# Staggered start addresses modulo 128 bytes for weight slots and activation tiles

## The chip, the cores and the metric

The kernel runs on one NeuronCore of one Trainium2 chip. The metric is the device time of one launch, in microseconds (us), taken as the median of several runs. Five engines take part: PE (TensorE, matrix products, with the loads of its stationary operand listed apart as PEld), DVE (VectorE), ACT (ScalarE), POOL (GpSimd) and SP (SyncE, which here only issues DMAs). A matmul reads two operands from SBUF: the stationary one (`lhsT`), which is loaded first, and the moving one (`rhs`), which is then streamed through.

## The reference

Two layers of a transformer block on 256 tokens with 1,024 features. Every layer is: half a SwiGLU feed-forward block, three mixers side by side (a gated MLP, a retention and a sparse attention), and a second half feed-forward block. Cut to what matters:

```python
def swiglu_ffn(x, w1, w2):
    a, b = jnp.split(x @ w1, 2, axis=-1)
    return (jax.nn.silu(a) * b) @ w2

for l in range(DEPTH):                                   # 2 layers
    x = x + 0.5 * swiglu_ffn(rms_norm(x, ffn1_norm[l]), ffn1_w1[l], ffn1_w2[l])
    h = rms_norm(x, mix_norm[l])
    proj = h @ w_in[l]                                   # 1024 -> 3864
    ...                                                  # y_a, y_b, y_c: the three mixers
    mix = g_a * (y_a @ w_out[0]) + g_b * (y_b @ w_out[1]) + g_c * (y_c @ w_out[2])
    x = x + mix @ w_o[l]
    x = x + 0.5 * swiglu_ffn(rms_norm(x, ffn2_norm[l]), ffn2_w1[l], ffn2_w2[l])
return rms_norm(x, final_norm)
```

The feed-forward width is 2,816 (22 blocks of 128). All is float32.

## The kernel before

Activations stand with the features on the 128 partitions and the 256 tokens along the free axis. To keep float32 accuracy on a faster matmul form (`float32r`), each factor is split in two: `hi` is its value rounded to float32r, `lo` what is left over. A product is then three matmuls: weight-hi by activation-hi, weight-hi by activation-lo, weight-lo by activation-hi.

**Weights.** `issue` (L206) brings the weights in pieces of up to 128 x 1024 floats: SP issues the DMA into a slot `raw` (4 slots of 4,096 bytes per partition), ACT copies it to `hi` (L219), and DVE and POOL share the subtraction that gives `lo` (L223). Both halves lie in one slot `hl` (4 slots of 8,192 bytes per partition: `hi`, then `lo` 4,096 bytes on). `piece` (L229) hands a piece out and keeps three more on their way.

**Activations.** `x16` (L112) gives a tile `xhl` for eight blocks of 128 features, `hi` first and `lo` 8,192 bytes on (2 slots of 16,384 bytes); the normed input of every stage lies in one. `s8` (L105) gives a tile for four blocks (6 slots of 8,192 bytes; the profile calls them `s`): the hidden blocks of the feed-forward, the mixers' outputs and several scratch tiles.

**Matmul helpers.** All of them go through `mm` (L147), so the profile puts all of them at L148.
- `mm_feat` (L240): stationary a weight block of 128 columns, moving 256 tokens; three matmuls of 256 columns per block.
- `mm_wide` (L259): the same with the two matmuls that share weight-hi taken as one of 512 columns, whose moving operand has two rows of 256 (`hi` and `lo`); so one matmul of 512 and one of 256 per block. Most of the feed-forward runs so.
- `mm_tok` (L274): the roles are swapped: stationary are 128 tokens of the activation, moving are the weights, 256 or 280 columns at a time. In `tok` (L902) with 280 columns a weight block begins every 280 x 4 = 1,120 bytes in its slot, and the pieces hold 3, 3 and 2 blocks; every block is used for both halves of the tokens, three matmuls each.
- `hidden` (L616): stationary are 60 columns of a scratch tile, moving are weights, two rows of 128.

**Order.** PE's instructions stand in the order in which the program writes them; the other engines' order is set by the scheduler. Small steps of the mixers (`unit`, `compress`, `retention` and others) are generators that run between the large products.

**Where tiles begin.** The allocator puts the slots of a pool one behind the other. By the built program, these are the places (start modulo 128 bytes) at which they begin:

| tile | slots | before | after |
|---|---|---|---|
| `raw` | 4 | 32 32 32 32 | the same |
| `hl` | 4 | 32 32 32 32 | 32 64 96 0 |
| `xhl` | 2 | 64 64 | 64 96 |
| `s` (by `s8`) | 6 | 64 64 64 64 64 64 | 0 32 64 96 0 32, each with 0 or 16 more by turns |
| `ph` | 2 | 96 96 | 96 96 |
| `ks` | 1 | 64 | 64 |

The 128-column blocks of a weight piece (512 bytes), the 256-token blocks of an activation (1,024 bytes) and the distances from `hi` to `lo` are multiples of 128 bytes, so they begin at their tile's place. The 280-column blocks don't: their three blocks begin at 32, 0 and 96 modulo 128.

Of the kernel before, what the change touches and what calls it, by code (L numbers as in the profile page):

```python
# [7 lines left out]
F32 = mybir.dt.float32  # L8
F32R = mybir.dt.float32r
# [12 lines left out]
GS = 0.21145921592590802  # L22
W2_SPLIT = (8, 8, 6)
SLOT = 1024

AHEAD = 3
FFN_SPLIT = 7
# [39 lines left out]
def tile_hybrid_block(  # L67
# [22 lines left out]
    ring = ctx.enter_context(tc.tile_pool(name="ring", bufs=1))  # L90
    act = ctx.enter_context(tc.tile_pool(name="act", bufs=1))
    ps = ctx.enter_context(tc.tile_pool(name="ps", bufs=1, space=PSUM))
    ctx.enter_context(tc.manual_schedule(engines={mybir.EngineType.PE}))
    uid = [0]

    def nm(s):
        uid[0] += 1
        return f"{s}_{uid[0]}"
# [4 lines left out]
        return t  # L103

    def s8(dt=F32R):  # L105
        return act.tile([128, 2, 4, 256], dt, tag="s8", name=nm("s8"), bufs=6)

    def flat8(dt=F32):
        t = s8(dt)
        return [t[:, i].rearrange("p a b -> p (a b)") for i in range(2)]  # L110

    def x16():  # L112
        return act.tile([128, 2, 8, 256], F32R, tag="xhl", name=nm("xhl"), bufs=2)

    def t2(tag="t2", bufs=6):
        return act.tile([128, 512], F32, tag=tag, name=nm(tag), bufs=bufs)

    def small(n, tag="small", bufs=17):
        return act.tile([128, n], F32, tag=tag, name=nm(tag), bufs=bufs)

    def pmm():
        return ps.tile([128, 512], F32, tag="mm", name=nm("mm"), bufs=2)

    def psc():
        return ps.tile([128, 512], F32, tag="sc", name=nm("sc"), bufs=3)
# [4 lines left out]
    def pms():  # L130
        return ps.tile([128, 512], F32, tag="ms", name=nm("ms"), bufs=2)

    def soon():

        return tc.high_priority(offset=EARLY)
# [11 lines left out]
    def mm(o, lhsT, rhs, start, stop):  # L147
        nc.tensor.matmul(o, lhsT=lhsT, rhs=rhs, start=start, stop=stop)  # L148
        n = 1
        for d in rhs.shape[1:]:  # L150
            n *= d
        if lhsT.dtype == F32R:
            clk[0] += max(n / 2400.0, 0.107) + 0.0025
        else:
            clk[0] += max(4 * n / 2400.0, 0.214)

    def transpose(o, i):
        nc.tensor.transpose(o, i, ident)  # L158
        clk[0] += 0.109
# [46 lines left out]
    def issue(cuts=1, between=None):  # L206
        kn, n = specs[len(queue)]
        raw = ring.tile([128, SLOT], F32, tag="raw", name=nm("raw"), bufs=4)
        hl = ring.tile([128, 2, SLOT], F32R, tag="hl", name=nm("hl"), bufs=4)
        hi, lo = hl[:, 0], hl[:, 1]  # L210
        o, m = woff[0], kn * n
        woff[0] += 128 * m
        src = w[o:o + 128 * m].rearrange("(p f) -> p f", p=128)
        for c in range(cuts):
            if between:
                between(c)
            s_ = slice(c * m // cuts, (c + 1) * m // cuts)
            nc.sync.dma_start(raw[:, s_], src[:, s_])
            S.copy(hi[:, s_], raw[:, s_])  # L219
            cut = m if cuts > 1 else (kn * pool_lo[0] // 8) * n  # L220
            for e, a, b in ((V, s_.start, min(cut, s_.stop)), (G, max(cut, s_.start), s_.stop)):
                if a < b:
                    e.tensor_tensor(out=lo[:, a:b], in0=raw[:, a:b], in1=hi[:, a:b].bitcast(F32), op=ALU.subtract)  # L223
        w3 = hl[:, :, :m].rearrange("p c (k n) -> p c k n", n=n)
        queue.append([w3[:, :, k] for k in range(kn)])
# [81 lines left out]
    def norm_begin(i):  # L307
        st = {"i": i, "n": 0, "q": []}
        if i < 6:
            hl = x16()  # L310
            st["h"], st["l"] = hl[:, 0], hl[:, 1]
            st["a"] = [hl[:, :, k] for k in range(8)]
        st["acc"] = act.tile([128, 256], F32, tag="acc", name=nm("acc"), bufs=1)
        return st
# [75 lines left out]
    def ffn(st, nxt, first=False, load=None):  # L390
# [3 lines left out]
        def evac(j, p):  # L394
            R2 = st["R"][:, None, :].to_broadcast([128, 2, 256])
            if j % 4 == 0:
                t4[:] = [s8()]
            h4, l4 = t4[0][:, 0], t4[0][:, 1]
            t, u = t2(), t2()
            t3 = t.rearrange("p (a b) -> p a b", a=2)  # L400
            if isinstance(p, list):
                for n in range(2):
                    S.copy(t3[:, n], p[n][:, 256:512])  # L403
                    V.tensor_tensor(out=t3[:, n], in0=p[n][:, 0:256], in1=t3[:, n], op=ALU.add)  # L404
                V.tensor_tensor(out=t3, in0=t3, in1=R2, op=ALU.mult)  # L405
            elif isinstance(p, tuple):
                for n in range(2):
                    V.tensor_tensor(out=t3[:, n], in0=p[n][:, 0:256], in1=st["R"], op=ALU.mult)
            else:
                V.tensor_tensor(out=t3, in0=p.rearrange("p (a b) -> p a b", a=2), in1=R2, op=ALU.mult)  # L410
            S.activation(u[:, 0:256], t[:, 0:256], AF.Silu)  # L411
            V.tensor_tensor(out=u[:, 256:512], in0=u[:, 0:256], in1=t[:, 256:512], op=ALU.mult)  # L412
            S.copy(h4[:, j % 4], u[:, 256:512])
            V.tensor_tensor(out=l4[:, j % 4], in0=u[:, 256:512], in1=h4[:, j % 4].bitcast(F32), op=ALU.subtract)  # L414
            hs.append(t4[0][:, :, j % 4])
# [91 lines left out]
    def mixer(l, st, nxt):  # L507
        a = st["a"]
# [38 lines left out]
        def has(*names):  # L547
            return lambda: all(n in ev for n in names)
# [167 lines left out]
        def cmp_branch(qt):  # L716
            yield has(f"s{qt}0", f"s{qt}1")
            sc = scs[qt]
            s3 = sc.rearrange("p (h n) -> p h n", n=16)
            mx = small(8)  # L720
            V.tensor_reduce(out=mx, in_=s3, axis=AX.X, op=ALU.max)
            V.tensor_tensor(out=s3, in0=s3, in1=mx[:, :, None].to_broadcast([128, 8, 16]), op=ALU.subtract)
            S.activation(sc, sc, AF.Exp)
            yield 2.0
            V.tensor_tensor(out=sc, in0=sc, in1=ccmp[:, 1, qt].rearrange("p j g n -> p (j g n)"), op=ALU.mult)
            sm = small(8)
            V.tensor_reduce(out=sm, in_=s3, axis=AX.X, op=ALU.add)
            V.tensor_scalar(sm, sm, 1e-30, None, op0=ALU.max)
            V.reciprocal(sm, sm)
            V.tensor_tensor(out=sm.rearrange("p (j g) -> p g j", g=2), in0=sm.rearrange("p (j g) -> p g j", g=2),  # L730
                            in1=gate[qt][:, :, 0].rearrange("p (g j) -> p g j", g=2), op=ALU.mult)
            V.tensor_tensor(out=s3, in0=s3, in1=sm[:, :, None].to_broadcast([128, 8, 16]), op=ALU.mult)
            yield WAIT_CB
            p = pms()
            transpose(p[:, 0:128], sc)
            ct = act.tile([128, 128], F32, tag="sct", name=nm("sct"), bufs=1)
            S.copy(ct, p[:, 0:128])
            yield 3.0
            yield has(f"u{qt}0", f"u{qt}1", "yalloc")
            o, p = os[qt], pms()  # L740
            for j in range(4):
                mm(p[:, j * 128:j * 128 + 128], lhsT=VC[:, j], rhs=ct, start=True, stop=True)
            qs = slice(qt * 128, qt * 128 + 128)
            o3 = o.rearrange("p (j t) -> p j t", j=4)
            with soon():
                V.tensor_tensor(out=o, in0=o, in1=p, op=ALU.add)
                S.copy(yh[2][:, :, qs], o3)
                V.tensor_tensor(out=yl[2][:, :, qs], in0=o3, in1=yh[2][:, :, qs].bitcast(F32), op=ALU.subtract)
            ev.add(f"yc{qt}")
# [270 lines left out]
        def outs(pairs, wks, alloc=pmm):  # L1020
            p = alloc()
            for n, (b, d) in enumerate(pairs):
                yield from mm_feat(p[:, n * 256:n * 256 + 256], wks[n], [yt[b][:, :, k] for k in range(4)], True, True)
            return p
# [3 lines left out]
        for d in range(8):  # L1028
# [6 lines left out]
            p = yield from outs(((0, d), (1, d)), (wk[0:4], wk[4:8]))  # L1035
# [14 lines left out]
        for d in range(0, 8, 2):  # L1050
# [10 lines left out]
            if d < 6:  # L1061
                p = yield from outs(((2, d), (2, d + 1)), (wk[0:4], wk[4:8]), psc)
# [6 lines left out]
            else:  # L1069
                u = t2()  # L1070
                for n in range(2):
                    p = yield from outs(((2, d + n),), (wk[4 * n:4 * n + 4],), psc)
# [8 lines left out]
        p = (pmm()[:, 0:256], psc()[:, 0:256])  # L1081
# [3 lines left out]
        for d in range(2, 8):  # L1085
            p = pmm()
            f, o = (mm_wide, p) if d < WIDE else (mm_feat, p[:, 0:256])
# [29 lines left out]
    for k, n in ((0, 1), (1, 2), (3, 2), (5, 2), (7, 1)):  # L1117
        t = t2()[:, 0:n * 256].rearrange("p (a b) -> p a b", b=256)
# [143 lines left out]
```

## Time and profile before

| | us |
|---|---|
| median of 3 runs (1267.82 to 1269.81) | 1268.05 |
| the profiled execution, its own time | 1271.46 |
| its span, first to last instruction | 1269.6 |
| PE busy in it | 1243.8 (98%) |
| DVE, ACT, POOL busy | 987.2, 718.6, 447.4 |

Busy time of PE counts a matmul from its start to its modelled end, and matmuls overlap, so a busy PE may still run at different paces. The pace is read from starts: from the start of one group of matmuls to the start of the next, divided by the matmuls in it.

### The profile page before, as it was taken

What the parts mean: (1) busy time and instruction counts of PE and PEld (TensorE: products, weight loads), DVE (VectorE), ACT (ScalarE), POOL (GpSimd) and SP (SyncE); (2) the same over time, 40 slices, a digit from 0 to 9 for tenths busy, and PEclk for the clock granted to TensorE, in tenths of its full rate; (3) what the DMA queues carried; (4) which work ended last, traced back from release to release, by engine and by line L of the source; (5) the groups of instructions that cost most, each with busy time, mean ns of one, the idle gap of its engine ahead of it and who ended that gap; (6) DMA issues with size and microseconds to landing.
All of it is one profiled execution on the core that took longest, in us unless ns stands there. A gap on an engine that the chain in (4) does not pass through costs nothing.

```text
span 1269.6 us, 22596 instructions
## 1 busy us (share of the span) xinstructions
PE 1243.8 (98%) x8440; PEld 1152.0 (91%) x8440; DVE 987.2 (78%) x1636; ACT 718.6 (57%) x1232; POOL 447.4 (35%) x419
## 2 busy tenths in 40 slices
PE   9999999998999999999999999999999999999997
PEld 9888899998998988888998888999999988888886
DVE  6988776789875888887778886686997758788863
ACT  6666445567764556564455654465676644666542
POOL 0533230264554733331213322203635548133222
PEclk9999999999998999999999999999999989999998
DMA  8855666644553555556555556575445545556562
GB/s 286 262 197 181 184 198 206 220 155 146 166 161 123 177 188 190 191 179 194 191 185 197 186 183 190 176 240 179 146 149 156 162 130 170 184 190 192 185 185 78
DMA packets 68957, 230.44 MB, mean 182 GB/s; under 512 B 8816, under 2 KB 11504, under 8 KB 68848
## 3 DMA queue, kind: packets, MB, share of 16 engines
q1 hardware_dynamic: 68256, 227.90, 55.8%
q0 software_dynamic: 448, 1.08, 0.3%
q8 instruction: 66, 1.08, 0.3%
q14 instruction: 43, 0.35, 0.1%
q10 hardware_dynamic: 144, 0.03, 0.0%
HBM read 225.80 MB, written 1.05 MB: 179 GB/s over the span
## 4 chain that ended last, share of the span: by engine, by line
PE 84%; DVE 5%; POOL 4%; ACT 3%; issue 2%; DMA 1%; SPq 0%; POOLq 0%; DVEq 0%; ACTq 0%
PE mm L148 58%; PE sc L148 23%; DVE hl L223 2%; PE ms L148 2%; POOL hl L223 1%; ACT hl L219 1%; POOL acc L345 1%; POOL sq L341 1%; PE o L148 1%; PE sc L158 1%; DMA raw<-in_w_dram 1%; ACT P L667 0%; ACT t L819 0%; DMA x<-in_x_dram 0%; POOL rs L794 0%
## 5 line engine op out<-in xcount | busy, mean ns | idle before, releaser
L223 DVE TENSOR_TENSOR hl<-raw,hl 128x896 fp32r<-128x896 f32 (+6 forms) x437 | 501.0, 1149 | 160.4 <-ACT hl L219 158.9
L219 ACT CAST hl<-raw 128x1024 fp32r<-128x1024 f32 (+3 forms) x437 | 443.5, 1018 | 283.7 <-PE mm L148 186.6
L148 PE MATMUL mm<-xhl,hl 128*128 128x256 f32 (+1 forms) x3784 | 561.0, 303 | 1.1 <-ACT hl L219 0.5
L148 PEld LDWEIGHTS mm<-xhl,hl 128*128 128x128 f32 x3784 | 507.5, 189 | 32.1 <-issue 1.4
L223 POOL TENSOR_TENSOR hl<-raw,hl 128x128 fp32r<-128x128 f32 (+2 forms) x264 | 309.1, 1172 | 487.3 <-ACT hl L219 458.1
L148 PE MATMUL mm<-s,hl 128*128 128x512 f32 (+1 forms) x1880 | 294.7, 317 | 0.0
L148 PEld LDWEIGHTS mm<-s,hl 128*128 128x128 f32 x1880 | 266.3, 188 | 25.9
L148 PE MATMUL sc<-xhl,hl 128*128 128x256 f32 (+1 forms) x1560 | 275.3, 328 | 0.1
L148 PEld LDWEIGHTS sc<-xhl,hl 128*128 128x128 f32 x1560 | 232.9, 189 | 25.9 <-DVE hl L223 0.3
L403 ACT COPY t<-sc 128x256 f32<-128x256 f32 x81 | 30.3, 374 | 90.3 <-PE sc L148 90.3
L341 POOL TENSOR_TENSOR sq<-x 128x256 f32<-128x256 f32 x36 | 25.0, 696 | 134.7 <-DVE x L386 134.7
L148 PE MATMUL mm<-hl,xhl 128*128 128x256 f32 (+1 forms) x432 | 59.9, 289 | 0.0
L405 DVE TENSOR_TENSOR t<-t,R 128x512 f32<-128x512 f32 x81 | 56.2, 694 | 2.8
L414 DVE TENSOR_TENSOR s<-t,s 128x256 fp32r<-128x256 f32 x88 | 56.7, 645 | 0.0
L148 PEld LDWEIGHTS mm<-hl,xhl 128*128 128x128 f32 x432 | 54.5, 188 | 2.2 <-issue 1.9
L345 POOL TENSOR_TENSOR acc<-acc,sq 128x256 f32<-128x256 f32 x36 | 51.6, 1433 | 2.0
L411 ACT ACTIVATE t<-t 128x256 f32<-128x256 f32 x88 | 36.7, 418 | 25.8 <-DVE t L405 24.9
L386 DVE SCALAR_TENSOR_TENSOR x<-mm,x 128x256 f32<-128x256 f32 x84 | 35.5, 423 | 15.5 <-PE mm L148 14.2
L320 DVE SCALAR_TENSOR_TENSOR xhl<-x,gnorm,xhl 128x256 fp32r<-128x256 f32 x48 | 39.4, 832 | 5.4 <-ACT xhl L319 5.4
L667 ACT ACTIVATE P<-P,small 128x128 f32<-128x128 f32 (+1 forms) x64 | 28.9, 452 | 25.9 <-DVE small L663 25.1
L404 DVE TENSOR_TENSOR t<-sc,t 128x256 f32<-128x256 f32 x81 | 34.4, 424 | 7.5 <-ACT t L403 3.4
L412 DVE TENSOR_TENSOR t<-t,t 128x256 f32<-128x256 f32 x88 | 37.4, 426 | 0.5 <-ACT t L411 0.5
(184 smaller groups left out, 854.0 us busy)
## 6 DMA issues: line engine op xcount, KB each, us to landing
raw<-in_w_dram SPq DMA_DIRECT2D x389, 512.0 KB, 3.5
raw<-in_w_dram SPq DMA_DIRECT2D x32, 384.0 KB, 3.0
raw<-in_w_dram SPq DMA_DIRECT2D x4, 420.0 KB, 3.1
x<-in_x_dram SPq DMA_DIRECT2D x4, 256.0 KB, 4.1
raw<-in_w_dram SPq DMA_DIRECT2D x8, 128.0 KB, 4.0
s<-in_c_alibi_dram SPq DMA_DIRECT2D x2, 512.0 KB, 7.3
lng<-in_lnp_dram SPq DMA_DIRECT2D x2, 512.0 KB, 4.1
ks<-ks POOLq DMA_DIRECT2D x4, 256.0 KB, 4.7
```

Of the source, the lines that this page charges most:

```text
L148: nc.tensor.matmul(o, lhsT=lhsT, rhs=rhs, start=start, stop=stop)
L219: S.copy(hi[:, s_], raw[:, s_])
L223: e.tensor_tensor(out=lo[:, a:b], in0=raw[:, a:b], in1=hi[:, a:b].bitcast(F32), op=ALU.subtract)
L320: V.scalar_tensor_tensor(st["l"][:, k], xs[k], g, st["h"][:, k].bitcast(F32), op0=ALU.mult, op1=ALU.subtract)
L341: (V if last else G).tensor_tensor(out=q, in0=xs[k], in1=xs[k], op=ALU.mult)
L345: (V if last else G).tensor_tensor(out=st["acc"], in0=st["acc"], in1=q, op=ALU.add)
L386: V.scalar_tensor_tensor(xs[d], p[:, i:i + 256], 0.5, xs[d], op0=ALU.mult, op1=ALU.add)
L404: V.tensor_tensor(out=t3[:, n], in0=p[n][:, 0:256], in1=t3[:, n], op=ALU.add)
L405: V.tensor_tensor(out=t3, in0=t3, in1=R2, op=ALU.mult)
L411: S.activation(u[:, 0:256], t[:, 0:256], AF.Silu)
L412: V.tensor_tensor(out=u[:, 256:512], in0=u[:, 0:256], in1=t[:, 256:512], op=ALU.mult)
L414: V.tensor_tensor(out=l4[:, j % 4], in0=u[:, 256:512], in1=h4[:, j % 4].bitcast(F32), op=ALU.subtract)
```

## The change

Slots of `hl`, `xhl` and `s` get 8 floats (32 bytes) of padding at their end, so that each slot begins 32 bytes further on modulo 128 than the one ahead of it. `s8` also shifts the part of its slot that is used by 4 floats (16 bytes) in every second call. To find the room, the tile `sct` of 512 bytes is given up; its one user, `cmp_branch`, writes the transposed scores back over the tile `scc` that the transpose has just read.

On every engine the instructions and their order stay as they are. Only addresses differ, and the copy at L736 (four times in all) now writes `scc`, which the 16 matmuls behind it read in place of `sct`.

```diff
+PAD_W, PAD_X, PAD_S = 8, 8, 8
...
+    turn = [0]
...
     def s8(dt=F32R):
-        return act.tile([128, 2, 4, 256], dt, tag="s8", name=nm("s8"), bufs=6)
+        t = act.tile([128, 2048 + PAD_S], dt, tag="s8", name=nm("s8"), bufs=6)
+        turn[0] = 4 - turn[0]
+        return t[:, turn[0]:turn[0] + 2048].rearrange("p (i a b) -> p i a b", i=2, a=4)
...
     def x16():
-        return act.tile([128, 2, 8, 256], F32R, tag="xhl", name=nm("xhl"), bufs=2)
+        t = act.tile([128, 4096 + PAD_X], F32R, tag="xhl", name=nm("xhl"), bufs=2)
+        return t[:, 0:4096].rearrange("p (i a b) -> p i a b", i=2, a=8)
...
-        hl = ring.tile([128, 2, SLOT], F32R, tag="hl", name=nm("hl"), bufs=4)
+        hl = ring.tile([128, 2 * SLOT + PAD_W], F32R, tag="hl", name=nm("hl"), bufs=4)
+        hl = hl[:, 0:2 * SLOT].rearrange("p (c f) -> p c f", c=2)
...
-            ct = act.tile([128, 128], F32, tag="sct", name=nm("sct"), bufs=1)
+            ct = sc
```

## Rows read from the trace of the kernel before

**Rows 1.** The page, parts 1 and 2: busy time by engine, and PE by slices.
```profile
PE 1243.8 (98%) x8440; PEld 1152.0 (91%) x8440; DVE 987.2 (78%) x1636; ACT 718.6 (57%) x1232; POOL 447.4 (35%) x419
...
PE   9999999998999999999999999999999999999997
...
PEclk9999999999998999999999999999999989999998
```
**Rows 2.** PE's waits: who waited for whom, us in all, times, longest.
```profile
PE sc L148 <- ACT s L747: 5.0, 2, 2.5
PE ms L148 <- DVE acc L345: 2.9, 2, 1.5
```
**Rows 3.** The chain that ended last: start us, us, what; projections, hidden blocks, last w2.
```profile
219.36 0.93 PE ms L148 x8
220.29 5.60 PE mm L148 x48
...
1198.62 53.41 PE mm L148 x308
```
**Rows 4.** Timeline of PE, layer 0, 280-column matmuls: start us, us to modelled end, count.
```profile
204.64 0.55 PE L148 MATMUL sc<-hl,xhl 128*128 128x280 f32 x3
...
205.41 0.54 PE L148 MATMUL sc<-hl,xhl 128*128 128x280 f32 x3
...
206.17 0.55 PE L148 MATMUL sc<-hl,xhl 128*128 128x280 f32 x3
...
206.94 0.55 PE L148 MATMUL sc<-hl,xhl 128*128 128x280 f32 x3
...
207.72 0.54 PE L148 MATMUL sc<-hl,xhl 128*128 128x280 f32 x3
...
208.48 0.55 PE L148 MATMUL sc<-hl,xhl 128*128 128x280 f32 x3
...
209.25 0.55 PE L148 MATMUL sc<-hl,xhl 128*128 128x280 f32 x3
...
210.02 0.54 PE L148 MATMUL sc<-hl,xhl 128*128 128x280 f32 x3
...
210.79 0.99 PE L148 MATMUL mm<-xhl,hl 128*128 128x256 f32 x7
```
**Rows 5.** The same stretch of layer 1.
```profile
829.45 0.55 PE L148 MATMUL sc<-hl,xhl 128*128 128x280 f32 x3
...
830.22 0.54 PE L148 MATMUL sc<-hl,xhl 128*128 128x280 f32 x3
...
830.98 0.55 PE L148 MATMUL sc<-hl,xhl 128*128 128x280 f32 x3
...
831.76 0.55 PE L148 MATMUL sc<-hl,xhl 128*128 128x280 f32 x3
...
832.53 0.54 PE L148 MATMUL sc<-hl,xhl 128*128 128x280 f32 x3
...
833.29 0.55 PE L148 MATMUL sc<-hl,xhl 128*128 128x280 f32 x3
...
834.06 0.55 PE L148 MATMUL sc<-hl,xhl 128*128 128x280 f32 x3
...
834.84 0.54 PE L148 MATMUL sc<-hl,xhl 128*128 128x280 f32 x3
...
835.60 0.64 PE L148 MATMUL mm<-xhl,hl 128*128 128x256 f32 x4
```
**Rows 6.** Timeline of PE: 256-column matmuls with moving weights, and what starts next.
```profile
257.77 6.20 PE L148 MATMUL mm<-hl,xhl 128*128 128x256 f32 x51
263.81 0.43 PE L148 MATMUL sc<-ks,xhl 128*128 128x288 f32 x2
```

## The prediction

> **What bounds the kernel now.** I read four views, in this order. First the busy times: PE is busy for 1243.8 us of a span of 1269.6, in every slice but a few, at its full clock [rows 1]. The next engine, DVE, has 22% to spare. Then PE's own waits: the two largest kinds come to 5.0 and 2.9 us over the whole run, so PE hardly ever stands [rows 2]. So the time is the number of matmuls times the pace at which PE starts them. The change leaves every instruction and its place as it is; it can act only through what an address costs. The third view is therefore the pace. In the chain, 48 matmuls of 256 columns take 5.60 us, 116.7 ns each [rows 3]; 256 columns at 2.4 GHz are 106.7 ns, so each has 10.0 ns on top. The last w2 stage runs 308 matmuls, 154 pairs of 512 and 256 columns, in 53.41 us, 346.8 ns a pair [rows 3], where 768 columns are 320.0 ns: 26.8 on top. With 8,104 float32r matmuls in the program, about 10 to 15 ns each, some 100 us lie above the pure streaming time. The question is whether start addresses have to do with it.
>
> The fourth view answers that in part, since one stretch of the kernel before already has staggered starts: the 280-column products. Stationary is an activation that begins at 64 modulo 128, moving is a weight block that begins at 32, then 0, then 96, in pieces of 3, 3 and 2 blocks, six matmuls per block. From the starts of groups of six [rows 4, 5]:
> - moving at 0: 0.76, 0.76, 0.77 in layer 0 and 0.76, 0.76, 0.76 in layer 1, together 4.57 us for 36 matmuls, **126.9 ns** each;
> - moving at 32: 0.77, 0.78, 0.77 and 0.77, 0.77, 0.78, together 4.64 us for 36, **128.9 ns**;
> - moving at 96: 0.77, 0.77 and 0.78, 0.77, together 3.09 us for 24, **128.8 ns**.
> Starts are given to 0.01 us, so a mean over 24 or 36 is good to some 0.3 ns. The difference of 2.0 ns stands in both layers. 280 columns are 116.7 ns, so the place 0 has 10.2 ns on top, just what the 256-column matmuls have whose moving operand begins at 64; the places 32 and 96 have 12.1. A second place agrees: with moving weights at 32, 51 matmuls of 256 columns take 257.77 to 263.81, 6.04 us, 118.4 ns each [rows 6], 1.7 more than with the moving operand at 64. I read this as: **a moving operand that begins on a multiple of 64 bytes runs at 10 ns on top, one that begins 32 past it at about 12.** Where the stationary operand begins seems not to matter: 64 in the 280s, 32 in the 48 matmuls, every multiple of 16 in the 60-column products, where eight matmuls with a moving operand at 32 take 0.93 us, 116.3 ns [rows 3], if anything less than the 118.4.
>
> The Trainium skill ("SBUF — State Buffer", Specifications (TRN2)) speaks of cachelines of 16 bytes, with a penalty for each crossing to a new one. By that grain every start here, before and after, is a whole line, and the change would cost nothing; the 2.0 ns of the 280s say that a coarser grain counts as well.
>
> **The change, part by part.** In the kernel before, 7,572 of the 8,104 float32r matmuls have a moving operand that begins on a multiple of 64 bytes (all that stream `xhl`, `s` or `ks`); 532 don't (508 with moving weights, 24 with `ph`). After, 2,552 do and 5,552 don't. By kind, the matmuls that newly lose the place:
> - 256 columns from `xhl`: 2,880 of 3,968 (the slot at 96, which serves both mixers and the second feed-forward of each layer);
> - 256 columns from `s`: 1,200 of 1,456;
> - two rows of 256 from `xhl` and `s`: 672 of 1,376 and 504 of 616, together 1,176;
> - moving weights go the other way, since two of four slots now begin on 64: 236 fewer.
>
> Single rows: 2,880 + 1,200 = 4,080 matmuls at 1.7 to 2.0 ns [rows 4 to 6] are 6.9 to 8.2 us. Two-row matmuls: the trace has none off the place. At least one row's price, 1.7 ns, at most one for each row, 4.0: 2.0 to 4.7 us. I take one price and a part, about 2.5 ns, 2.9 us, since the second row follows the first without a new instruction. Moving weights: 236 at 2.0 give back 0.5 us. Middle of the first, 7.6, plus 2.9, less 0.5: **10.0 us**; the ends are 6.9 + 2.0 - 0.5 = 8.4 and 8.2 + 4.7 - 0.4 = 12.5.
>
> Of the 5,552, 1,104 begin 16 or 48 past a multiple of 64, which no moving operand does before. The nearest rows are those 32 past; bounded by nothing and by twice that, they change the sum by 1,104 x 2 ns, 2.2 us down or up. I take the rows' value and keep both ends: 6 to 15 us.
>
> All of it lies on the path: PE is in order, and hardly anything else holds it up. PE's waits total little, so a slower PE has little to give back; where PE waits for weights it takes the loss in, some tenths of a us.
>
> *The stationary operand* now begins at four places rather than one. By the 60-column products and the 280s I cost this at nothing; its bound is the spread between rows that differ in it, some 0.4 ns of 116.7 either way, 3 us over 8,104.
>
> *The other engines* write and read the same tiles at new places. Before, DVE, ACT and POOL already work on tiles at 0, 32, 64 and 96; DVE's 22% [rows 1] and the three pieces of weights that lie ahead of PE cover small changes. I cost them at nothing. If the cover failed, it would show as new waits of PE for `hl`.
>
> *The tile `sct`*: the copy now writes `scc`, and must wait for the transpose to have read it. It waits for that transpose's result anyway. Four copies, nothing.
>
> Sum: the profiled execution's own time of 1271.46 would become 1281.5. It lies 3.4 above the median of the runs, 1268.05, so the median becomes **1278.0**, 0.8% slower.
>
> **The rivals.** *Faster: it is the distance between the two operands that counts, not the moving start.* In the 280s the slow places lie 32 from the stationary start (32 and 96 against 64), the fast one 64 from it. Before, 7,472 matmuls stand at a distance of 32; after, they are spread, and 1,730 more than before stand at 64, 2,314 with the neighbours 48 and 80. At 2.0 ns each that is 3.5 to 4.6 us less: 1264.0. It decides from 0.3 ns a matmul on. For it: the 280s fit, and if two reads can collide, one common distance is where they would. Against it: the 48 matmuls at a distance of 32 have 10.0 ns on top [rows 3], the 280s at that distance 12.1 and at 64 10.2 [rows 4, 5]; by distance alone 32 would have two prices, and what 64 has to offer the 48 have already. The Trainium skill ("TensorE: Matmul & The Clock Gate", Step-by-step: what each phase is for) gives the two operands separate read ports, so that loading the next weights takes nothing from the running matmul, which speaks against a collision too.
>
> *The same: the 2 ns belong to the product with swapped roles, not to the address.* All rows off the place have weights as moving operand; if activations don't mind, nothing moves and the time stays at 1268. Against it: within the 280s the roles are the same and only the start differs. For it: the 60-column products, with a moving start of 32, run at 116.3, no slower than the 48. The 16-byte grain that the Trainium skill states ("SBUF — State Buffer", Specifications (TRN2)) would give this time as well.
>
> **How the numbers follow.** A measurement of this kernel tells about 0.2% from no change, 2.5 us. The forecast, slower, gets 0.54: its rows are the only ones in which nothing but a start differs, but they are few. Faster gets 0.24, the same 0.22. The predicted time is 1278. The forecast alone spans 1274 to 1283. To hold 8 in 10 the range must take in the same (1265.5 to 1270.5) and the price of the faster rival, 1263.4; its top is the upper sum of 15 with a margin of 1: 1262 to 1284.
>
> **What would show it.** The instruction counts stay and PE's busy time grows by about 10 us. The 48 matmuls at 220 us, whose `xhl` slot moves to 96, take 5.68 to 5.70 in place of 5.60, while the first feed-forward of either layer, whose slot stays at 64, keeps its pace in w1. The pairs of the last w2 stage, from 53.41, take 53.7 to 54.1. The 280s no longer step by thirds alike in every piece, since their slots differ. The forecast is wrong if those 48 keep 5.60 or fall below it, or if PE's pace stays and new waits for `hl` carry the time.

## The result, and the profile after

The changed kernel takes 1276.07 us (median of 4 runs, 1274.92 to 1277.39) against 1268.5 for the kernel before (4 runs): a ratio of 1.0059, 95% interval 1.0041 to 1.0076. It is slower by 7.6 us; the prediction said 1278 and slower.

The page of the kernel after, from parts 1 and 2, as in [rows 1]:

```profile
PE 1247.2 (98%) x8440; PEld 1148.8 (90%) x8440; DVE 988.3 (78%) x1636; ACT 717.8 (56%) x1232; POOL 445.6 (35%) x419
...
PEclk9999999999998999999999999999999999999999
```

PE stays the bound with the same number of instructions, and PE's waits keep their size: the largest is the same one as in [rows 2], and all that the view lists come to 19.3 us in either kernel.

```profile
PE sc L154 <- ACT s L754: 5.0, 2, 2.5
```

What changed is PE's pace. The chain that ended last, in order of time (start us, us, what): first three groups of 48 single matmuls of 256 columns in layer 0's mixers (single: not half of a pair of 512 and 256 columns), then the last w2 stage, to be held against [rows 3].

```profile
200.51 5.67 PE mm L154 x48
...
221.85 5.58 PE mm L154 x48
...
232.85 5.62 PE mm L154 x48
...
1201.71 53.98 PE mm L154 x308
```

The 154 pairs of the last w2 stage take 53.98 us, 350.5 ns a pair, where they took 346.8: 3.7 ns more, 0.6 us in this stage alone. The singles run at 118.1, 116.3 and 117.1 ns, where all three groups ran at 116.7: some lose and one gains. Taken over the whole trace, from each start to the next, 1,985 pairs average 350.2 ns against 346.8 before, and some 3,150 singles of weights by activations 117.9 against 117.2. With 1,992 pairs and 3,432 singles in the program that is an estimated 6.8 us in the pairs and 2.4 in the singles, a little more than the 7.6 measured. So most of the loss sits in the pairs of `mm_wide`, and not only in those whose moving operand moved. The timeline of PE in the first feed-forward's w1 shows that (start us, us to the modelled end, 16 matmuls in 8 pairs to a row); there `xhl` begins at 64 modulo 128 in both kernels. Before:

```profile
62.28 2.94 PE L148 MATMUL sc<-xhl,hl 128*128 128x512 f32 x16
65.06 2.94 PE L148 MATMUL mm<-xhl,hl 128*128 128x512 f32 x16
67.83 2.94 PE L148 MATMUL sc<-xhl,hl 128*128 128x512 f32 x16
70.60 2.94 PE L148 MATMUL mm<-xhl,hl 128*128 128x512 f32 x16
73.38 2.94 PE L148 MATMUL sc<-xhl,hl 128*128 128x512 f32 x16
```

After:

```profile
62.23 2.97 PE L154 MATMUL sc<-xhl,hl 128*128 128x512 f32 x16
65.03 2.95 PE L154 MATMUL mm<-xhl,hl 128*128 128x512 f32 x16
...
73.41 2.97 PE L154 MATMUL sc<-xhl,hl 128*128 128x512 f32 x16
```

From the first start to the last, 32 pairs take 11.10 us before (346.9 ns each) and 11.18 after (349.4). Only the weight slots have moved here. By the prediction's reading, these pairs should have kept their pace.

One caution on the totals: the two profiled executions differ by 3.5 us (1271.46 and 1274.92), the medians by 7.6. In the execution of before, PE's granted clock stood at its lower level for a while in two late stretches; in the one after it didn't. The first of them by stretch (us, busy time of each engine with its instructions, then the granted clock as a share of full, DMA share, GB/s), before:

```profile
1023.00:1031.00 8.00, 6.85 (x32) 6.56 (x33) 2.33 (x3) 1.55 (x3) 0.58 (x2) 0.57 0.22 66
```

After:

```profile
1023.00:1031.00 8.00, 4.85 (x37) 4.35 (x36) 5.57 (x7) 4.11 (x7) 2.65 (x2) 1.00 0.43 131
```

In the 7 us ahead of it (1016 to 1023) PE had been busy for 5.17 us before, and for all 7 after. The second stretch, 1078 to 1082, shows 0.57 and 1.00 as well. A mean of 0.57 means that 86% of these 12 us ran at the lower of the two levels, 1.2 GHz, about 10 us in which half the work was done: some 5 us that the execution of before paid and the one after did not. That is also why PE's busy time grew by 3.4 us only, from 1243.8 to 1247.2. Paces below are therefore taken from rows at full clock, and times from medians.

### The profile page after: what moved, and what is told of

Read it like the earlier page. It is cut to its first block, busy times and chain, and to the rows that moved or that the text cites. A ratio compares the mean times of both kernels' runs of the same rounds, so it can differ in the third digit from the quotient of the medians.

```text
span 1273.1 us, 22596 instructions
## 1 busy us (share of the span) xinstructions
PE 1247.2 (98%) x8440; PEld 1148.8 (90%) x8440; DVE 988.3 (78%) x1636; ACT 717.8 (56%) x1232; POOL 445.6 (35%) x419
## 4 chain that ended last, share of the span: by engine, by line
PE 85%; DVE 5%; POOL 4%; ACT 3%; issue 2%; DMA 0%; POOLq 0%; DVEq 0%; ACTq 0%
PE mm L154 59%; PE sc L154 23%; DVE hl L230 2%; PE ms L154 2%; POOL hl L230 1%; ACT hl L226 1%; POOL acc L352 1%; POOL sq L348 1%; PE o L154 1%; PE sc L164 1%; ACT P L674 0%; DVE small L677 0%; DMA gnorm<-in_norms_dram 0%; DVE s L479 0%; DVE t L477 0%
```

## The experiments

All compare with the kernel before on the same chip. Distance means: start of the moving operand less start of the stationary one, modulo 128 bytes; whether 128 is enough is a question that the second group of runs below answers. In the kernel before the distance is 32 for nearly all matmuls of weights by activations. Every run gives up `sct` as the change does, also where the lines shown leave that out. Theory M is the prediction's (what counts is whether the moving start is a multiple of 64), theory D says that the distance counts, theory S that turning from place to place costs.

### Everything moved on by 32 bytes, distances kept

```diff
-    fold = const.tile([128, 30], F32, tag="fold", name="fold")
+    fold = const.tile([128, 38], F32, tag="fold", name="fold")[:, 0:30]
...
-            ct = act.tile([128, 128], F32, tag="sct", name=nm("sct"), bufs=1)
+            ct = sc
```

> Every tile that matmuls read lies 32 bytes further on (and sct is given up, as in the change), so all distances between the two operands stay as in the kernel before: 32 for almost all float32r matmuls. The moving operand now begins at 96 modulo 128, 32 past a multiple of 64. Theory M of the prediction (the moving start counts, on a multiple of 64 or not): 7,400 matmuls lose the place, at 1.7 to 2 ns each and the two-row ones up to twice that, so 1280 to 1285 us. Theory D (the distance between moving and stationary start counts): as before, 1268.5 us within 1.5, and 346.8 ns a pair in the last w2 stage. A change of the time would also be what giving up sct costs, if it costs anything.

Measured: 1269.21 us, ratio 1.0006 (0.9996 to 1.0015). No change, and the same pace to the hundredth in the chain:

```profile
219.75 5.59 PE mm L148 x48
...
1196.67 53.41 PE mm L148 x308
```

Theory M falls: 7,572 moving operands left their multiple of 64, 532 others came onto one, and nothing happened. The 280-column matmuls show it in the rows. Here the stationary operand begins at 96 and the three moving blocks at 64, 32 and 0, so the block at a distance of 64 is the one that begins at 32. Timeline of PE, one row for each start of a block:

```profile
204.09 0.55 PE L148 MATMUL sc<-hl,xhl 128*128 128x280 f32 x3
...
204.86 0.54 PE L148 MATMUL sc<-hl,xhl 128*128 128x280 f32 x3
...
205.62 0.55 PE L148 MATMUL sc<-hl,xhl 128*128 128x280 f32 x3
...
206.40 0.55 PE L148 MATMUL sc<-hl,xhl 128*128 128x280 f32 x3
...
207.17 0.54 PE L148 MATMUL sc<-hl,xhl 128*128 128x280 f32 x3
...
207.93 0.55 PE L148 MATMUL sc<-hl,xhl 128*128 128x280 f32 x3
...
208.70 0.55 PE L148 MATMUL sc<-hl,xhl 128*128 128x280 f32 x3
...
209.48 0.54 PE L148 MATMUL sc<-hl,xhl 128*128 128x280 f32 x3
...
210.24 0.99 PE L148 MATMUL mm<-xhl,hl 128*128 128x256 f32 x7
```

Blocks that begin at 32 take 0.76, 0.76 and 0.76, 126.7 ns a matmul; those at 64 and 0 take 0.77, 0.77, 0.78 and 0.78, 0.77, 129.0 ns. The fast place went with the distance: in [rows 4, 5] it began at 0, here it begins at 32, and the starts on a multiple of 64 are now the slow ones. The run also says that giving up `sct` costs nothing that can be measured.

### One distance for all, seven other values

The weight slots are made 128 bytes longer, which leaves all slots alike modulo 128 (though not modulo 256, which matters below), and the part of each that is used begins o floats into it (o = 24 for a distance of 64, 8 for 0, 16 for 96, 4 for 16, 28 for 48, 12 for 112, 20 for 80); activations stay at 64. `sct` is given up as in the change.

```diff
-        hl = ring.tile([128, 2, SLOT], F32R, tag="hl", name=nm("hl"), bufs=4)
+        hl = ring.tile([128, 2 * SLOT + 32], F32R, tag="hl", name=nm("hl"), bufs=4)
+        hl = hl[:, o:o + 2 * SLOT].rearrange("p (c f) -> p c f", c=2)
```

Distance 64:

> All weight slots begin alike at 0 modulo 128, the activations stay at 64: one distance of 64 for almost all matmuls, no staggering. Theory M: the moving operands keep their place, so no change, 1268.5 us. Theory D, with the prices that the trace of the changed kernel shows by distance: pairs of 512 and 256 columns take 350 to 352 ns at 64 against 348 at 32 there, so 1,992 pairs by 2 to 4 ns are 4 to 8 us more; single 256-column matmuls take 115.5 to 117.8 against 118.0, so some 3,300 of them by 0.2 to 2.5 are 1 to 8 us less. Together 1265 to 1276 us, with the pairs slower and the singles faster. Theory S (it is the turning of places from slot to slot that costs, any one distance is as good): 1268.5 us and the same pace of pairs and singles as before.

Distance 0:

> All weight slots begin at 64 modulo 128 like the activations: one distance of 0. Theory M: 1268.5 us. Theory S: 1268.5 us. Theory D, with the prices of the changed kernel: pairs 350.8 against 348.0 ns, 1,992 of them are 5.6 us; singles 118.6 to 119.0 against 118.0, 3,300 of them are 2 to 3.3 us: 1276 to 1278 us.

Distance 96:

> All weight slots begin at 96 modulo 128, the activations stay at 64: one distance of 96 (32 the other way). Theory M and theory S: 1268.5 us. Theory D, with the prices of the changed kernel: pairs 350.7 against 348.0 ns, 5.4 us; singles 119.65 against 118.0, 3,300 of them are 5.4 us: 1279 us. If distance counted without its sign, it would be as before, 1268.5 us.

Distance 16:

> All weight slots begin at 48 modulo 128, the activations at 64: one distance of 16. Theory D, with the prices in the trace of the changed kernel, where single tiles at 16 show pairs of 346.7 to 348.5 ns against 348.2 at 32, and singles of 115.7 to 118.0 against 118.0: pairs 0 to 1.5 ns cheaper than at 32 (0 to 3 us), singles 0 to 2 (0 to 7 us): 1259 to 1269 us, the first uniform distance that may be below the kernel before. A theory by which only multiples of 32 are good places for the stationary operand: 1275 us or more.

Distance 48:

> All weight slots begin at 16 modulo 128: one distance of 48. Theory D, with the changed kernel's prices: pairs at 48 of 348.8 to 350.7 ns against 348.2 at 32 (1 to 5 us more), singles of 119 against 118 (3 us more): 1272 to 1277 us.

Distance 112:

> All weight slots begin at 80 modulo 128: one distance of 112, that is 16 the other way. Theory D, with the changed kernel's prices: pairs of 349.4 to 351.0 ns against 348.2 at 32 (2 to 6 us more), singles of 117.7 against 118.0 (0 to 1 us less): 1270 to 1275 us. If the distance counted without its sign, the same as at 16.

Distance 80:

> All weight slots begin at 112 modulo 128, the activations at 64: one distance of 80, the last multiple of 16. Theory D, with the prices in the trace of the changed kernel, where single tiles at 80 show the dearest pairs of all, 353.9 against 348.5 ns at 32, and singles of 118.7 against 118.0: pairs 5 to 7 ns dearer than in the kernel before (10 to 14 us), singles 1 to 2 (3 to 6 us): 1281 to 1288 us. But cells of the changed kernel have been off by up to 3 ns for the uniform distances 16 and 64, so anything from 1276 us up would not be against it; at or below 1270 us would be.

The chain of each, the group of 48 singles at about 220 us and the 154 pairs of the last w2 stage. Distance 0:

```profile
222.77 5.72 PE mm L148 x48
...
1210.88 54.05 PE mm L148 x308
```

16:

```profile
221.91 5.75 PE mm L148 x48
...
1208.06 53.98 PE mm L148 x308
```

48:

```profile
222.22 5.65 PE mm L148 x48
...
1206.40 54.15 PE mm L148 x308
```

64:

```profile
222.73 5.56 PE mm L148 x48
...
233.61 5.46 PE mm L148 x48
...
853.06 5.65 PE mm L148 x48
...
1205.48 54.38 PE mm L148 x308
```

80:

```profile
221.03 5.67 PE mm L148 x48
...
1202.40 53.62 PE mm L148 x308
```

96:

```profile
222.69 5.71 PE mm L148 x48
...
1209.08 54.14 PE mm L148 x308
```

112:

```profile
221.07 5.71 PE mm L148 x48
...
1202.43 53.70 PE mm L148 x308
```

Divided by 154 and by 48, with the measured times:

| distance | us, median | ratio (95%) | ns a pair | ns a single |
|---|---|---|---|---|
| 0 | 1283.53 | 1.0112 (1.0095 to 1.0128) | 351.0 | 119.2 |
| 16 | 1280.34 | 1.0085 (1.0068 to 1.0101) | 350.5 | 119.8 |
| 32 (all moved by 32) | 1269.21 | 1.0006 (0.9996 to 1.0015) | 346.8 | 116.5 |
| 48 | 1279.58 | 1.0082 (1.0067 to 1.0097) | 351.6 | 117.7 |
| 64 | 1277.43 | 1.0068 (1.0053 to 1.0083) | 353.1 | 113.8 to 117.7 |
| 80 | 1275.13 | 1.0042 (1.0026 to 1.0059) | 348.2 | 118.1 |
| 96 | 1282.41 | 1.0108 (1.0093 to 1.0123) | 351.6 | 119.0 |
| 112 | 1276.99 | 1.0062 (1.0046 to 1.0079) | 348.7 | 119.0 |

The distance sets the pace. Theory M, which gave 1268.5 for distances 0, 64 and 96, is out. So is a theory that only the stationary operand's own start counts: it is 64 modulo 128 in the kernel with everything moved and in the one at distance 0, and they take 1269.21 and 1283.53 us. The kernel before stands at the best of the eight, and the pairs, over half of PE's time (1,992 by 346.8 ns are 691 us), are cheapest there; singles are on average cheapest at 64 (116.2 ns over the whole trace, against 117.2 before and 117.8 to 119.1 at the other distances), where pairs are dearest. The sign counts: 32 and 96, or 16 and 112, are not alike.

**128 bytes is not the whole period.** The slots of these seven kernels lie 8,320 bytes apart, so each begins 128 bytes further on modulo 256 than the one ahead of it. The first feed-forward's w1 takes its pieces of 8 pairs from the slots in turn; at distance 16 (timeline of PE, one piece to a row):

```profile
61.96 2.98 PE L148 MATMUL sc<-xhl,hl 128*128 128x512 f32 x16
64.78 2.94 PE L148 MATMUL mm<-xhl,hl 128*128 128x512 f32 x16
67.57 2.98 PE L148 MATMUL sc<-xhl,hl 128*128 128x512 f32 x16
70.39 2.94 PE L148 MATMUL mm<-xhl,hl 128*128 128x512 f32 x16
```

The pieces take 2.82, 2.79 and 2.82 us, 352.5 and 348.8 ns a pair by turns; over the whole trace, with the places of the built program, pairs from `xhl` that lie 16 apart modulo 256 average 347.7 ns and those that lie 144 apart 353.3. The kernel before, which writes to `sc` and `mm` by turns as well, shows no such step in the rows above: its slots are alike modulo 8,192. So each line of the table, but for that of 32, is a mean over two distances 128 bytes apart. At 32 the two are the same: by the built program pairs from `xhl` lie 32 apart modulo 256 in the kernel before and those from `s` 160, and they average 346.8 and 346.7 ns. Slots 256 bytes apart agree to 0.1 ns at distance 16, which points to a period of 256; no run tests that by itself.

Theory S needs care for the same reason, since modulo 256 the seven kernels do turn. What rules it out is a stage of a later run, the one with the activations alone staggered: in the second feed-forward's w1 all weight slots are alike as in the kernel before, only the `xhl` slot lies 32 bytes further on, nothing turns, and 32 pairs take 11.31 us, 353.4 ns each, where they took 346.8.

```profile
470.37 2.98 PE L152 MATMUL sc<-xhl,hl 128*128 128x512 f32 x16
...
481.68 3.00 PE L152 MATMUL sc<-xhl,hl 128*128 128x512 f32 x16
```

None of the seven expected times held. Six kernels came out above what the prices read off single tiles of the changed kernel promised, by 1.4 us (64) to 11 (16: at most 1269 promised, 1280.34 measured), and 80 came out 6 below (1281 or more promised, 1275.13 measured). Prices from a kernel with mixed distances, sorted modulo 128, did not carry over. A rough sum, 1,992 pairs and 3,432 singles at the differences of the table, gives 17.0 us for distance 0 (14.2 measured, from the ratio) and 9.5 for distance 64 (8.6, with its group of 115.8), but 18.0 for distance 16 (10.8): one group of singles does not stand for all. With the means over all pairs and singles of each trace the same sum gives 14.6, 8.7 and 13.6 us, and 11.5 for 48 (10.4 measured), 6.3 for 80 (5.3), 15.2 for 96 (13.7) and 8.4 for 112 (7.9): a little high, and in nearly the right order.

### The two halves of the change

Weight slots staggered alone:

```diff
-        hl = ring.tile([128, 2, SLOT], F32R, tag="hl", name=nm("hl"), bufs=4)
+        hl = ring.tile([128, 2 * SLOT + 8], F32R, tag="hl", name=nm("hl"), bufs=4)
+        hl = hl[:, 0:2 * SLOT].rearrange("p (c f) -> p c f", c=2)
```

> One part of the change alone: the four weight slots are staggered (32, 64, 96, 0), xhl and s all stay at 64, so the distances 32, 0, 96 and 64 come up in turn. Theory D: about the mean of the four uniform kernels measured so far, (1268.9 + 1283.5 + 1282.4 + 1277.4) / 4 = 1278.1 us, within 2. Theory M of the prediction: 1268 us, since the moving places stay. If turning from slot to slot had a price of its own, above 1280.

Measured: 1276.58 us, ratio 1.0057 (1.0042 to 1.0072), as slow as the whole change, without one activation moved modulo 128. The mean of the four uniform kernels, 1278.1, fits within the 2 us that were allowed; theory M gave 1268.

Activations staggered alone (the lines of the change for `s8`, `x16` and `turn`, weights as before):

```diff
+        t = act.tile([128, 2048 + 8], dt, tag="s8", name=nm("s8"), bufs=6)
+        turn[0] = 4 - turn[0]
+        return t[:, turn[0]:turn[0] + 2048].rearrange("p (i a b) -> p i a b", i=2, a=4)
...
+        t = act.tile([128, 4096 + 8], F32R, tag="xhl", name=nm("xhl"), bufs=2)
+        return t[:, 0:4096].rearrange("p (i a b) -> p i a b", i=2, a=8)
```

> The other part of the change alone: xhl and s are staggered as in the change, the four weight slots stay alike at 32. Theory D: pairs from xhl, 676 of them (the second feed-forwards) go from a distance of 32 to 64, at 352.9 in place of 346.8 ns, 4.1 us more; about 500 of the pairs from s go to mixed distances, some 4 ns, 2 us more; the 2,112 singles of the mixers go to 64, 0.9 to 1.6 ns, 1.9 to 3.4 us less; moving weights 0.7 less; so 1.5 to 3.5 us more, 1270.5 to 1272.5 us. Theory M: this part carries the whole loss of the change, 1276 us or more.

Measured: 1274.14 us, ratio 1.0046 (1.0033 to 1.0059): above the 1270.5 to 1272.5 of theory D, below the 1276 of theory M. The chain says where the gain in the mixers stayed out:

```profile
199.37 5.44 PE mm L152 x48
...
220.10 5.65 PE mm L152 x48
...
1201.38 53.97 PE mm L152 x308
```

Both groups of 48 read the mixers' input at a distance of 64 (by the built program modulo 512 too), yet one runs at 113.3 ns and the other at 117.7, as do most of those behind it. So one distance can hold two paces.

The halves lose 0.57% and 0.46%, the whole 0.59%. They don't add, which is what theory D asks for: each half alone already spreads the distances, and spreading them twice leaves them spread. The mean ratio of the eight uniform kernels is 1.0071, the change's 1.0059.

### The price list used: singles at 64, pairs at 32

```diff
-    def x16():
-        return act.tile([128, 2, 8, 256], F32R, tag="xhl", name=nm("xhl"), bufs=2)
+    def x16(o=0):
+        t = act.tile([128, 4096 + 32], F32R, tag="xhl", name=nm("xhl"), bufs=2)
+        return t[:, o:o + 4096].rearrange("p (i a b) -> p i a b", i=2, a=8)
...
-            hl = x16()
+            hl = x16(8 if i % 3 == 1 else 0)
...
-            ct = act.tile([128, 128], F32, tag="sct", name=nm("sct"), bufs=1)
+            ct = sc
```

> The kernel before, but the tile that holds the mixers' normed input begins 32 bytes further on (96 in place of 64 modulo 128). Its 2,112 single matmuls and 420 moving-weight matmuls then have a distance of 64, and all pairs keep 32. Theory D, with the paces of the uniform kernels: singles 116.2 at 64 (115.5 in the changed kernel) against 117.1 at 32, so 0.9 to 1.6 ns each, 1.9 to 3.4 us less; moving weights 116.9 against 118.5, 0.7 us less; sum 2.6 to 4.1 us less, 1265 to 1266.5 us: faster than both kernels by 0.2 to 0.3% of the kernel before. Theory M of the prediction: the same tile loses its place, 2,112 by 1.7 to 2 ns, 3.6 to 4.2 us more, 1273 us.

Measured: 1264.8 us (12 runs) against 1268.57 (17 runs), ratio 0.9976 (0.9965 to 0.9986): 3 to 4 us faster than the kernel before, and so faster than both.

```profile
218.95 5.46 PE mm L149 x48
...
402.34 5.65 PE mm L149 x48
...
1192.04 53.40 PE mm L149 x308
```

Most groups of these singles run at about 113.8 ns where they ran at 116.7, some, such as that at 402.34, at 117.7; the pairs keep their 346.8. Modulo 128 the edit is 32 bytes in one tile, in the direction that theory M calls wrong. Both `xhl` slots grow by 128 bytes, though, so by the built program the mixers' input lies 192 from the weights modulo 256 here and 64 in the run before this one. That may be why more groups take the faster pace here; no run moves this tile by 128 bytes alone.

## Why the prediction was right, and where it was not

**Right: the bound and the path.** The prediction held that only PE's pace can move, that it passes to the end undiminished, and that the other engines and `sct` cost nothing. PE's waits did not grow, and the run with everything moved shows no price of `sct`.

**Right: that starts matter, and that the change loses.** The direction came out as forecast. The 2 ns between places in the 280-column rows are real; the run moved by 32 shows them again at other addresses.

**Wrong: the step from those rows to "a moving operand on a multiple of 64".** The 280s fit that and fit the distance as well. I chose by one comparison: 256-column matmuls at a distance of 32 had 10.0 ns on top, 280-column ones at that distance 12.1, so "by distance alone 32 would have two prices". The tacit step is that one price list serves all shapes. It doesn't: pairs are cheapest at 32 and dearest at 64, singles on average cheapest at 64. The same step put the stationary operand's place at nothing, with 3 us either way as its bound; the weight slots staggered alone lose 7.5 us, as much as the whole change. The rival had the right variable, up to its period, and the wrong prices; it priced every matmul by the 280s and left out the pairs, which the trace showed only at a distance of 32, so that nothing in it could say what they would do elsewhere.

**The size came out near in good part by luck.** I had 4,080 matmuls of 256 columns at 1.7 to 2.0 ns carrying 7.6 of the 10 us, and the 512-column ones 2.9. The 4,080 take in the second matmul of 1,176 pairs, so by the forecast the pairs carry about 5.1 us (1,176 by 1.9 and 2.5 ns) and 2,904 singles 5.4. Measured, 1,992 pairs, more than were thought to lose, by 2.5 ns (from `xhl` in the first feed-forward) to 3.7 (from `s`) are 5.0 to 7.4 us, most of the loss, and the singles gain at some distances and lose at others. The group of 48 singles, forecast at 5.68 to 5.70, came to 5.58. The prediction had named this as a sign of its failure: "if those 48 keep 5.60 or fall below it". The w1 stage that should have kept its pace lost 2.5 ns a pair. The w2 pairs at 53.98 lie in the forecast 53.7 to 54.1, for a cause that was not the one given.

**Rival "faster"** (3.5 to 4.6 us less by distance): the gain for singles exists, as the last experiment shows with 3 to 4 us, when the pairs are left at 32. **Rival "the same"**: its ground, that activations don't mind where they begin, holds in the run with everything moved; what it left out is the distance, by which the first feed-forward's w1 lost 2.5 ns a pair.

**What was read beside the rows.** The 16-byte grain that the Trainium skill gives ("SBUF — State Buffer", Specifications (TRN2)), taken as the only one, would have made the change free; here starts that are all multiples of 16 differ by up to 1.1% of the kernel's time. The 16-byte grain of the Trainium skill may hold for one operand alone, which the run with everything moved agrees with (ratio 1.0006); what the distance between two operands costs, it leaves open. The separate read ports of "TensorE: Matmul & The Clock Gate" (the Trainium skill, Step-by-step: what each phase is for) I took as speaking against any effect of the distance; the effect is there, so as a ground it did not carry.

**Open.** The distance is shown to be a variable that sets the pace; its full period (more than 128 bytes) and why it counts are not. A collision between the read of the moving operand and the load of the next stationary one would depend on the distance, but no run here separates the two reads. Nor is it settled what picks between the two paces that singles show at a distance of 64, nor why the paces of a kernel with mixed distances differ from those of one with a single distance.

## What to carry to other kernels

Where PE is the bound, look at the pace of starts, not at the busy share, and treat the start of the moving operand less that of the stationary one as a number to tune for each shape: here it is worth up to 1.1% one way and 0.2% the other. Note it modulo 256 bytes or more, since places that agree modulo 128 can still differ. Equal places in all slots are not a fault; staggering them only trades one distance for a mixture, which is worse when that one was good. Before calling a kernel uniform, see that its pieces run at one pace. And when two readings fit the rows, price the shape that has most of the time before choosing, or say that no row shows it.

## What the runs showed of the hardware that was not expected

- Moving both operands of the float32r products on by 32 bytes changes nothing (1.0006), moving one against the other by 32 changes 0.7 to 1.1%.
- Places that agree modulo 128 bytes can differ: pairs whose operands lie 16 and 144 apart run at 347.7 and 353.3 ns in one execution.
- Singles at the same distance can settle at two paces, 113.3 and 117.7 ns, in one execution.
- The best distance depends on the shape: 32 for pairs of 512 and 256 columns (346.8 ns, against 353.1 at 64), 64 for single 256-column matmuls (116.2 on average, against 117.2 at 32).
